# Two-block transformer kernel: the input rows of the first layer are scaled on ScalarE instead of VectorE

## Chip, core and metric

The kernel runs on one core of a Trainium2 chip. The metric is device time of one execution in microseconds. A row of the profile names engines as PE (TensorE), PEld (TensorE's weight loads), DVE (VectorE), ACT (ScalarE), POOL (GpSimd) and SP (the engine that issues the DMAs).

## What is computed

Two blocks follow each other on 1024 tokens of width 1024. The first has two layers. Its layer 0, where the change is, works on the 1024 rows of `x` and 256 context rows `ctx`:

```
hx = rms_norm(x, norm_g[layer]) * (1.0 + scx[:, None, :]) + shx[:, None, :]
hc = rms_norm(ctx, norm_g[layer]) * (1.0 + scc) + shc
...
ox, oc = even_mixer(hx, hc, ...)        # window attention with sinks, differential attention
x = x + gtx[:, None, :] * (ox @ w_out[layer])
```

with

```
def rms_norm(x, g):
    xf = x.astype(jnp.float32)
    y = xf * lax.rsqrt(jnp.mean(xf * xf, axis=-1, keepdims=True) + EPS)
    return (y * g.astype(jnp.float32)).astype(x.dtype)
```

`scx` and `shx` come from the condition through `adaln_params`. Layer 1 is gated linear attention. The second block mixes an LRU, a forgetting attention and an RWKV group, and ends with a gated feed-forward. All data are fp32.

## The kernel before

Rows are cut into tiles of 128: eight of `x` (t = 0 to 7) and two of `ctx` (t = 8, 9). Matrix products are made of fp32r halves: `split` (lines 99 to 106) casts a tile to a high part and subtracts it for the low part, and `mm3` (lines 126 to 134) runs three matmuls for each of eight slices of 128 (L132, L133, L134).

For each of the ten tiles `in_rows` (line 262) loads the rows into `x` (L266), squares two halves on ScalarE with a running sum (L270), adds the two sums on VectorE (L272), and calls `rsqrt`: multiply and add on VectorE (L95), power -0.5 on GpSimd (L97). L274 multiplies the whole 128x1024 tile by that value, in place. `in_T` (line 277) transposes it on TensorE in two halves (L258), evicts with the adaLN scale and shift, on ScalarE for the first half (L289) and on VectorE for the second (L287), and splits into `hT` (the cast, L105 on VectorE or L103 on ScalarE) and `lo` (L106 on GpSimd). The buffers `xt` are two, shared with `jk`, the output of the squares.

`keys_values` (line 548) multiplies a tile's `hT` with the first weights (`whi`, `wlo`; result in `mm`), norms and rotates the keys (`kn`, L358 to L375), transposes them (L382) and stores `kT` and `v`. `window_group` (line 466) takes four head pairs over the ten tiles: `proj_qg` makes q and its gate (`gs`, L430, L431), then scores (L394), row maxima (L400), exponentials (L601), transposed weights (L408, L410), and the sum over values (L615). The first four input tiles (8, 9, 0, 1) are prepared in `build`, between the adaLN products (L149 to L161); the rest by `ready` as pair 0 reaches them. Later adaLN parts (L179, L182, L187) run on ScalarE and GpSimd beside the window attention. `differential_group` follows. Line 249 in `norm_rows` is a scaling like L274 that already runs on ScalarE; it is used much later.

Nobody writes the order of instructions by hand here: the tile framework is called with its scheduler on (`schedule_with_timeline_sim=True`), which lays out each engine's queue from its own estimate of durations. Each engine then takes its queue strictly in that order. So an edit of one instruction can change the order on all engines, and in stages that follow.

Of the kernel before, what the change touches and what calls it, by code (L numbers as in the profile page):

```python
# [15 lines left out]
AF = mybir.ActivationFunctionType  # L16
ALU = mybir.AluOpType
# [14 lines left out]
class Builder:  # L32
# [229 lines left out]
    def in_rows(self, t):  # L262

        nc, I = self.nc, self.I
        x = self.adp.tile([128, 4, 256], F32, tag="x", name="x").rearrange("p a b -> p (a b)")
        nc.sync.dma_start(x, I["x"][t * 128:(t + 1) * 128] if t < 8 else I["ctx"][(t - 8) * 128:(t - 7) * 128])  # L266
        ss, rs = self.sums()
        jk = self.adp.tile([128, 512], F32, tag="xt", name="jk", bufs=XT)
        for half in range(2):
            nc.scalar.activation(jk, x[:, half * 512:half * 512 + 512], AF.Square, accum_out=ss[:, half:half + 1])  # L270
        rs = rs[:, :1]
        nc.vector.tensor_tensor(rs, ss[:, 0:1], ss[:, 1:2], op=ALU.add)  # L272
        self.rsqrt(rs, rs, 1.0 / 1024, EPS, 1)
        nc.vector.tensor_scalar(x, x, rs, None, op0=ALU.mult)  # L274
        return x

    def in_T(self, t, x, mds):
# [1788 lines left out]
```

## Time and profile before

| | us |
|---|---|
| median of 3 runs | 3123.26 |
| lowest, highest | 3115.8, 3126.36 |
| profiled execution, own time | 3118.71 |
| span of that execution | 3116.9 |
| TensorE busy | 2994.9 (96%) |
| VectorE busy | 2001.0 (64%) |
| ScalarE busy | 1451.7 (47%) |
| GpSimd busy | 749.7 (24%) |

The first tile's squares begin at 13.5 us, the last scaling of L274 at 130.0 us; the last value product of the window attention (L615) begins at 426.4 us. In the rows below, times are microseconds from the start of the span. A timeline row gives start, duration, engine, line, operation, output and inputs, and in brackets the idle time just before it and who ended it.

### The profile page before, as it was taken

What the parts mean: (1) busy time and instruction counts of PE and PEld (TensorE: products, weight loads), DVE (VectorE), ACT (ScalarE), POOL (GpSimd) and SP (SyncE); (2) the same over time, 40 slices, a digit from 0 to 9 for tenths busy, and PEclk for the clock granted to TensorE, in tenths of its full rate; (3) what the DMA queues carried; (4) which work ended last, traced back from release to release, by engine and by line L of the source; (5) the groups of instructions that cost most, each with busy time, mean ns of one, the idle gap of its engine ahead of it and who ended that gap; (6) DMA issues with size and microseconds to landing.
All of it is one profiled execution on the core that took longest, in us unless ns stands there. A gap on an engine that the chain in (4) does not pass through costs nothing.

```text
span 3116.9 us, 54778 instructions
## 1 busy us (share of the span) xinstructions
PE 2994.9 (96%) x20419; PEld 2729.3 (88%) x20419; DVE 2001.0 (64%) x5219; ACT 1451.7 (47%) x3605; POOL 749.7 (24%) x812
## 2 busy tenths in 40 slices
PE   8899999999999999999999999999998899999999
PEld 5799999889888789998788989888877899999887
DVE  5677757777776665446546543576645999998443
ACT  4689845555563553223236221245644444444332
POOL 2467621332220000000000000111002666663000
PEclk9999999999999999999999999899999999999999
DMA  5222210100033231112321121312232222223562
GB/s 216 61 87 85 93 41 5 33 28 13 15 129 115 87 111 58 50 56 85 122 84 48 51 71 56 89 47 60 71 111 82 68 82 89 82 82 114 175 198 95
DMA packets 164138, 253.00 MB, mean 81 GB/s; under 512 B 25800, under 2 KB 93440, under 8 KB 163872
## 3 DMA queue, kind: packets, MB, share of 16 engines
q1 hardware_dynamic: 163872, 249.50, 25.0%
q8 instruction: 161, 2.64, 0.4%
q14 instruction: 105, 0.86, 0.1%
HBM read 194.94 MB, written 54.51 MB: 80 GB/s over the span
## 4 chain that ended last, share of the span: by engine, by line
PE 80%; DVE 8%; DMA 4%; ACT 4%; issue 2%; POOL 1%; SPq 0%; DVEq 0%; POOLq 0%; ACTq 0%
PE mm L132 12%; PE mm L133 12%; PE mm L134 12%; PE dn L1788 8%; PE mm L1708 4%; PE mm L1707 4%; PE mm L1709 4%; PE te L408 3%; PE po L1537 3%; PE sc L394 3%; PE po L664 2%; PE po L615 2%; DVE upl L106 1%; ACT EB L649 1%; PE sc L885 1%
## 5 line engine op out<-in xcount | busy, mean ns | idle before, releaser
L132 PE MATMUL mm<-whi,hT 128*128 128x256 f32 (+1 forms) x1760 | 514.6, 293 | 18.4 <-DVE gs L431 5.4
L133 PE MATMUL mm<-wlo,hT 128*128 128x256 f32 (+1 forms) x1760 | 507.6, 289 | 1.9 <-POOL wlo L106 1.9
L132 PEld LDWEIGHTS mm<-whi,hT 128*128 128x128 f32 x1760 | 337.9, 192 | 26.2 <-DVE gs L431 5.6
L133 PEld LDWEIGHTS mm<-wlo,hT 128*128 128x128 f32 x1760 | 338.1, 192 | 5.3 <-POOL wlo L106 2.5
L134 PE MATMUL mm<-whi,lo 128*128 128x256 f32 x1040 | 301.1, 290 | 0.9 <-POOL lo L106 0.8
L97 POOL TENSOR_TENSOR inv<-inv,cm 128x1 f32<-128x1 f32 (+1 forms) x87 | 50.4, 580 | 1029.3 <-DVE inv L95 1029.3
L1653 POOL TENSOR_TENSOR uptmp<-upraw 128x256 f32<-128x256 f32 x220 | 216.2, 1011 | 231.9 <-DMA upraw<-in_ffn_up 219.0
L132 PE MATMUL mm<-hT,whi 128*128 128x352 f32 (+3 forms) x640 | 220.4, 345 | 2.8 <-ACT a L1021 1.8
L97 POOL TENSOR_TENSOR c<-c,cm 128x2 f32<-128x2 f32 (+1 forms) x170 | 126.3, 744 | 401.1 <-DVE c L95 355.6
L133 PE MATMUL mm<-hT,whi 128*128 128x352 f32 (+3 forms) x640 | 218.8, 342 | 0.1
L134 PE MATMUL mm<-hT,wlo 128*128 128x352 f32 (+3 forms) x640 | 218.6, 343 | 0.0
L410 ACT COPY wT<-te 128x512 f32<-128x512 f32 (+2 forms) x368 | 159.0, 453 | 121.0 <-PE te L408 110.8
L134 PE MATMUL mm<-whi,hT 128*128 128x256 f32 (+3 forms) x720 | 205.5, 286 | 0.0
L134 PEld LDWEIGHTS mm<-whi,lo 128*128 128x128 f32 x1040 | 202.3, 195 | 3.2 <-POOL lo L106 1.5
L1811 DVE SCALAR_TENSOR_TENSOR fy<-fx,ffnc,fy 128x512 f32<-128x512 f32 x176 | 135.7, 793 | 15.1 <-ACT fy L1809 15.1
L400 DVE TENSOR_SCALAR_CACHE_REDUCE EB<-sc 128x512 f32<-128x512 f32 (+1 forms) x208 | 120.0, 585 | 35.9 <-PE sc L394 33.1
L182 POOL TENSOR_TENSOR adacc<-adacc,adpr 128x512 f32<-128x512 f32 (+1 forms) x112 | 128.6, 1148 | 47.8 <-ACT adpr L179 32.3
L103 ACT CAST whi<-wraw 128x512 fp32r<-128x512 f32 (+2 forms) x120 | 84.0, 718 | 118.9 <-PE mm L133 45.4
L394 PE MATMUL sc<-kT,qTh 128*128 128x256 f32 (+2 forms) x352 | 125.8, 372 | 13.3 <-DVE EB L400 6.6
L1788 PE MATMUL dn<-dnl,fh 128*128 128x512 f32 x352 | 137.3, 390 | 0.0
L1788 PE MATMUL dn<-dnh,fl 128*128 128x512 f32 x352 | 137.2, 391 | 0.0
L134 PEld LDWEIGHTS mm<-whi,hT 128*128 128x128 f32 (+1 forms) x720 | 135.7, 188 | 1.4
(544 smaller groups left out, 9078.2 us busy)
## 6 DMA issues: line engine op xcount, KB each, us to landing
adraw<-in_adaln_w SPq DMA_DIRECT2D x48, 512.0 KB, 3.7
upraw<-in_ffn_up SPq DMA_DIRECT2D x44, 512.0 KB, 3.8
dnraw<-in_ffn_down SPq DMA_DIRECT2D x88, 256.0 KB, 3.4
wraw<-in_w_ab SPq DMA_DIRECT2D x26, 512.0 KB, 3.7
woraw<-in_w_out SPq DMA_DIRECT2D x48, 256.0 KB, 2.9
wraw<-in_w_gla SPq DMA_DIRECT2D x48, 256.0 KB, 2.8
wraw<-in_w_in SPq DMA_DIRECT2D x24, 512.0 KB, 4.2
fd<-fy SPq DMA_DIRECT2D x44, 256.0 KB, 2.5
```

What stands on the lines that cost most here:

```text
L97: nc.gpsimd.tensor_tensor(out, out, self.cm05[:p, :n], op=ALU.pow)
L132: mmul(ps, ah, bh, start=k == 0, stop=False)
L133: mmul(ps, ah, bl, start=False, stop=False)
L134: mmul(ps, al, bh, start=False, stop=k == nk - 1)
L182: nc.gpsimd.tensor_tensor(a, a, pr[:, :conds], op=ALU.add)
L394: self.nc.tensor.matmul(sp, q[x][:, m], keys, start=x == 0, stop=last and x == 1)
L410: nc.scalar.copy(w[:n, :m, :nq], ps.rearrange("p (j t) -> p j t", j=4)[:n, :m, :nq])
L1653: nc.gpsimd.tensor_tensor(tmp[:, qs], src, raw[:, h2, :, 128 * r2:128 * r2 + 128], op=ALU.add if sign > 0 else ALU.subtract)
L1707: nc.tensor.matmul(ps, wh, th, start=k == 0, stop=False)
L1708: nc.tensor.matmul(ps, wh, tl, start=False, stop=False)
L1788: nc.tensor.matmul(banks[t][i], a[e], b[g], start=k == 0 and n == 0, stop=k == 21 and n == 2)
L1811: nc.vector.scalar_tensor_tensor(y, x[part][:, :, tap:tap + 256], cw[:, tap, c:c + 1], y, op0=ALU.mult, op1=ALU.add)
```

## The change

L274 is one instruction. It was a `tensor_scalar` multiplication on VectorE; it becomes an activation with the function Copy and the per-row scale on ScalarE. Data, buffers and the steps around it stay.

```
@@ -271,7 +271,7 @@
         rs = rs[:, :1]
         nc.vector.tensor_tensor(rs, ss[:, 0:1], ss[:, 1:2], op=ALU.add)
         self.rsqrt(rs, rs, 1.0 / 1024, EPS, 1)
-        nc.vector.tensor_scalar(x, x, rs, None, op0=ALU.mult)
+        nc.scalar.activation(x, x, AF.Copy, scale=rs)
         return x
```

The order of instructions moves in four stretches: the whole window attention (762 of TensorE's rows), a few rows early in the differential attention, the forgetting attention of the second block (345 rows), and the start of the feed-forward (28 rows).

First place: ScalarE, between the adaLN products and the first keys. `xt` and `te` belong to the input tiles, `whi<-wraw` is a cast of weights, `adr` an adaLN row. Piece of the difference:

```order
 L289 ACTIVATE xt<-te,md_195 128x128 x2
 L289 ACTIVATE xt<-te,md_257 128x128 x2
+L274 ACTIVATE x<-x,inv 128x1024
 L103 CAST whi<-wraw 128x1024
 L152 COPY adr<-mm 2x512
+L103 CAST hT<-xt 128x4x128
 L103 CAST whi<-wraw 128x1024
-L103 CAST hT<-xt 128x4x128 x2
+L103 CAST hT<-xt 128x4x128
```

The scaling of tile 1 comes in ahead of a weight cast, and the first of two `hT` casts moves ahead of the next weight cast.

Second place: TensorE, after the keys of tile 1 (`mm_632`). `mm_677` and `mm_805` are q and gate of tiles 0 and 1, `te_736` and `te_748` the transposes of tile 2's rows `x_725`, `mm_760` tile 2's keys. Before:

```order
L134 MATMUL mm_632<-whi_205,lo11_122 128x256
L258 MATMUL te_736<-ident_r_68,x_725 128x128 x4
L258 MATMUL te_748<-ident_r_68,x_725 128x128 x4
L132 MATMUL mm_677<-whi_398,hT_118 128x256
L133 MATMUL mm_677<-wlo_399,hT_118 128x256
L134 MATMUL mm_677<-whi_398,lo00_119 128x256
```

And now:

```order
L134 MATMUL mm_677<-whi_404,lo01_120 128x256
L382 MATMUL tp_626<-ident_r_68,kn_612 128x128 x2
L258 MATMUL te_736<-ident_r_68,x_725 128x128 x4
L258 MATMUL te_748<-ident_r_68,x_725 128x128 x4
L382 MATMUL tp_671<-ident_r_68,kn_657 128x128 x2
L132 MATMUL mm_760<-whi_199,hT_118 128x256
L133 MATMUL mm_760<-wlo_200,hT_118 128x256
L132 MATMUL mm_805<-whi_398,hT_118 128x256
```

Tile 2's transposes moved behind the 24 matmuls of `mm_677`, and its keys were interrupted after two matmuls by `mm_805`.

Third place: TensorE in the forgetting attention, beside the RWKV group (`ra`). Before:

```order
L1184 MATMUL ra_21811<-X_21776,B_21378 128x128 x4
L1512 MATMUL sc_23874<-fkh_23776,fqh_23774 128x400
L1513 MATMUL sc_23874<-fkc0_23760,fql_23775 128x400
L1537 MATMUL po_23813<-fv_23783,wT_23816 16x64
L408 MATMUL te_23838<-ident_r_68,fE_23800 128x128
L1190 MATMUL ra_21834<-XT_21709,Y_21809 128x128 x4
```

And now:

```order
L1184 MATMUL ra_21811<-X_21776,B_21378 128x128 x4
L1537 MATMUL po_23813<-fv_23783,wT_23816 16x64
L408 MATMUL te_23838<-ident_r_68,fE_23800 128x128
L1512 MATMUL sc_23874<-fkh_23776,fqh_23774 128x400
L1513 MATMUL sc_23874<-fkc0_23760,fql_23775 128x400
L1190 MATMUL ra_21834<-XT_21709,Y_21809 128x128 x4
```

The same matmuls stand there; the scores of one query tile moved behind the value product of an earlier one.

## Rows read from the trace of the kernel before

**Rows 1.** The page: busy times, and the chain that ended last by engine.

```profile
PE 2994.9 (96%) x20419; PEld 2729.3 (88%) x20419; DVE 2001.0 (64%) x5219; ACT 1451.7 (47%) x3605; POOL 749.7 (24%) x812
...
PE 80%; DVE 8%; DMA 4%; ACT 4%; issue 2%; POOL 1%; SPq 0%; DVEq 0%; POOLq 0%; ACTq 0%
```

**Rows 2.** Busy us by stretch: from:to, length, PE, PEld, DVE, ACT, POOL, clock, DMA.

```profile
0.00:436.00 436.00, 401.16 (x3092) 370.47 (x3093) 287.96 (x1068) 309.31 (x957) 224.13 (x219) 0.97 0.31 102
...
1990.00:2320.00 330.00, 320.56 (x2204) 273.34 (x2204) 204.72 (x750) 170.25 (x420) 37.55 (x41) 0.95 0.28 77
...
48.00:61.00 13.00, 9.68 (x46) 9.41 (x47) 12.14 (x24) 7.03 (x25) 8.79 (x8) 0.63 0.53 175
61.00:75.00 14.00, 13.11 (x106) 12.58 (x105) 11.07 (x34) 6.94 (x32) 5.89 (x8) 0.98 0.13 43
75.00:100.00 25.00, 19.96 (x142) 18.62 (x142) 17.64 (x71) 15.24 (x51) 8.31 (x9) 0.91 0.15 46
100.00:135.00 35.00, 30.85 (x239) 29.24 (x238) 24.02 (x95) 20.73 (x71) 10.24 (x12) 0.97 0.13 44
```

**Rows 3.** TensorE's longest waits for VectorE, 0 to 200 us: total us, times, longest.

```profile
PE mm L132 <- DVE gs L431: 5.4, 3, 3.6
PE sc L394 <- DVE EA L400: 3.2, 2, 1.9
PE tp L382 <- DVE kn L358: 2.7, 1, 2.7
```

**Rows 4.** Line 274 by form (busy us, mean ns, idle before); line 249 (ns min/median/max).

```profile
L274 DVE TENSOR_SCALAR x<-x,inv 128x1024 f32<-128x1024 f32 x10 | 7.5, 753 | 5.4 <-POOL inv L97 5.4
...
L249 ACT ACTIVATE xs<-x,inv x9: 1147/1152/1153, 2298.1 to 2396.1; 128x1024 f32<-128x1024 f32 x8, 16x1024 f32<-16x1024 f32 x1
```

**Rows 5.** Timeline, end of tile 4's second square on ScalarE and its scaling.

```profile
84.70 0.19 ACT L270 ACTIVATION_READ_ACCUMULATOR jk<-x 128x1 f32 x1
...
85.94 0.75 DVE L274 TENSOR_SCALAR x<-x,inv 128x1024 f32<-128x1024 f32 x1 [0.67 <-POOL inv L97]
```

**Rows 6.** Timeline, 42 to 58 us: tiles 8 and 9, then kn.

```profile
42.82 1.37 DVE L287 TENSOR_SCALAR xt<-te,md 128x128 f32<-128x128 f32 x4
...
45.12 1.04 ACT L103 CAST whi<-wraw 128x1024 fp32r<-128x1024 f32 x1 [3.42 <-DMA wraw<-in_w_ab]
46.07 1.14 ACT L103 CAST hT<-xt 128x512 fp32r<-128x512 f32 x2
...
46.74 0.38 PE L132 MATMUL mm<-whi,hT 128*128 128x256 f32 x1 [1.84 <-ACT hT L103]
...
57.56 0.41 PE L382 MATMUL tp<-ident_r,kn 128*128 128x128 f32 x2 [2.72 <-DVE kn L358]
...
46.76 3.02 POOL L106 TENSOR_TENSOR lo<-xt,hT 128x512 fp32r<-128x512 f32 x2 [7.09 <-ACT hT L103]
53.45 1.73 POOL L106 TENSOR_TENSOR lo<-xt,hT 128x512 fp32r<-128x512 f32 x1 [3.67 <-DVE c L95]
...
55.93 0.29 DVE L375 TENSOR_TENSOR jk<-mm,c 128x128 f32<-128x128 f32 x1 [0.60 <-POOL c L97]
```

**Rows 7.** Timeline, tile 2 from its scaling to hT, and TensorE's wait at 73.78.

```profile
62.32 0.75 DVE L274 TENSOR_SCALAR x<-x,inv 128x1024 f32<-128x1024 f32 x1 [0.73 <-POOL inv L97]
...
65.27 1.04 PE L258 MATMUL te<-ident_r,x 128*128 128x128 f32 x8
...
67.83 0.42 DVE L105 CAST hT<-xt 128x512 fp32r<-128x512 f32 x1
...
73.78 0.35 PE L132 MATMUL mm<-whi,hT 128*128 128x256 f32 x1 [0.80 <-DVE gs L431]
```

**Rows 8.** ScalarE's longest wait in total, 40 to 135 us.

```profile
ACT jk L347 <- PE mm L134: 15.4, 8, 4.1
```

**Rows 9.** TensorE's two longest waits, 1990 to 2300 us.

```profile
PE ra L1213 <- ACT bn L1301: 3.0, 1, 3.0
PE sc L1512 <- DVE fkh L1480: 2.8, 1, 2.8
```

More of the change, by code (lines that the diff above doesn't have):

```diff
@@ L273, in in_rows @@
         self.rsqrt(rs, rs, 1.0 / 1024, EPS, 1)
-        nc.vector.tensor_scalar(x, x, rs, None, op0=ALU.mult)
+        nc.scalar.activation(x, x, AF.Copy, scale=rs)
         return x
```

## Prediction, made before the changed kernel ran

> **What bounds the kernel now.** I read the page first. TensorE is busy 96% of the span and carries 80% of the chain that ended last; VectorE carries 8%, ScalarE 4% [rows 1]. So an edit on VectorE or ScalarE counts only where TensorE waits for one of them, or where it moves TensorE's own work. The table by stage says where that can be. The ten edited instructions run between 16 and 130 us, inside the window attention of the first layer, which fills the first 436 us; TensorE idles 436 - 401.2 = 34.8 us of these [rows 2]. The list of TensorE's waits up to 200 us names whom it waited for: VectorE's lines 431, 400 and 358 for 11.3 us in all [rows 3]. The edited line 274 is in no row of it: TensorE never waited for a scaled row directly. What the edit can do goes through the queues of VectorE and ScalarE, and through the order in which the scheduler, which sees other durations, now lays out all engines.
>
> **What is removed.** Ten multiplications of 128x1024 on VectorE, 753 ns each, 7.5 us together. Before them VectorE sat 5.4 us idle in eight waits for the power on GpSimd, since the product stands straight behind the sum and the scaled mean that feed it [rows 4]. So VectorE gets back up to 7.5 + 5.4 = 12.9 us, of which the four early tiles (up to 40 us) are worth nothing: there TensorE works through the adaLN products and comes to the transposes later than their rows are scaled.
>
> **What is added.** Ten activations with a per-row scale on ScalarE. The trace has the same form, out of the same kind of buffers, at line 249: 1152 ns [rows 4]. That is 11.5 us, 0.40 us more than on VectorE for each tile. The order lists hold these ten more instructions on ScalarE and nothing else, so no table load comes with them. The wait for the power moves too. From the end of the second square's accumulator (84.70 + 0.19 = 84.89) to the scaling (85.94) it is 1.05 us on an idle VectorE [rows 5]. On ScalarE the scaling of three of the ten tiles (3, 6 and 7) stands straight behind its own squares, and blocks the queue for about those 1.05 us; the casts of q, the square sums of the keys and the exponentials stand behind it. The other seven have work in between.
>
> By the Trainium skill (ScalarE: Activation LUTs, Rules for kernel authors) a plain multiplication belongs on VectorE, and the two durations of [rows 4] agree for the single instruction. If each tile's extra 0.40 us were on the path the sum would be 4.0 us worse; the forecast's own terms below do not use this.
>
> **What moves, first place: 44 to 58 us.** Before, ScalarE's first hT cast waits behind a weight cast whose data land at 45.12. TensorE runs dry at 46.74 - 1.84 = 44.90 and starts again at 46.74; GpSimd then makes the two low halves in 1.51 us each, and TensorE stops 2.72 us more until VectorE's kn lets it go on at 57.56 [rows 6]. In the new order the first cast stands ahead of the weight cast. Its input is evicted half way through the row of 42.82, at about 43.5; with 0.57 us for the cast and 1.51 us for the low half tile 8 continues at about 45.6. Tile 9 still needs the weight cast, its own cast and its low half: 45.12 + 1.04 + 0.57 + 1.51 = 48.2. But all that TensorE then does is to reach the wait for kn earlier, and VectorE's list of work ahead of kn is the same as before. One thing changes there: the hT cast of tile 0 moves ahead of two evictions and two table products, so GpSimd's 1.73 us subtraction behind it ends sooner, by more than the 0.60 us for which line 375 waited on the power queued behind that subtraction. Gain: this 0.60 us, not the 1.84 us that a list of waits suggests.
>
> **Second place: 61 to 75 us.** Before, tile 2's row is scaled by 62.32 + 0.75 = 63.07 us, transposed from 65.27 on, and its hT cast ends at 67.83 + 0.42 = 68.25, 2.98 us after the transposes began [rows 7]. Now ScalarE scales it behind the square sums of tile 0's keys, and on TensorE the transposes stand 24 matmuls and two transposes later. A matmul takes 13.11 / 106 = 0.124 us in this stretch [rows 2]: 24 x 0.124 = 3.0, with the pair 3.2 us. So the transposes begin at 65.3 - 0.6 + 3.2 = 67.9 and hT is there at 70.9. TensorE has done the transposes (1.04 us) and the next pair (0.41) by 69.3 and waits 1.6 us for it. The wait of 0.80 us at 73.78 goes with the old order. Cost: 0.8 us. The two places together leave +0.2 us.
>
> **The other five tiles, 75 to 135 us.** VectorE gets 5 x (0.75 + 0.67) = 7.1 us back; ScalarE takes 5 x 1.15 + 3 x 1.05 = 8.9 us more. Both have room on average: in these 60 us ScalarE is idle 24.0 us and VectorE 18.3 us [rows 2]. Most of ScalarE's idle time is waiting for TensorE's products, 15.4 us between 40 and 135 us in eight waits of up to 4.1 us [rows 8], and that is what covers the added work. I take 0, with -7.1 and +8.9 as ends. If the cover is gone, the scaling is late for tp and scores and costs its 1.15 us a tile.
>
> **Later stages.** What the ramp has won or lost by 135 us is passed on: every stage after it is TensorE's [rows 1]. The forgetting attention of the second block has no edited instruction, but the scheduler ordered 345 of TensorE's rows there differently. Between 1990 and 2320 us TensorE idles 9.4 us, mostly in two waits of 3.0 and 2.8 us [rows 2, 9]. Such waits can vanish or come again: 0, with -5.8 and +5.8. The feed-forward start has 28 rows moved; I take 0.
>
> **Sum.** The profiled execution took 3118.71 us with a span of 3116.9. +0.2 makes 3118.9. The median of the three runs is 3123.26, 4.55 us above it, so the prediction is 3123.5 us. A measurement of this kernel tells about 0.3%, 9.4 us, from no change; the runs of before lie between 3115.8 and 3126.36.
>
> **The rivals.** (a) *ScalarE becomes the bound, slower.* Place: tiles 3 to 7, where casts of q and exponentials queue behind a scaling that waits for GpSimd. Price: 8.9 us there and 0.8 us at tile 2 without the gain at the first place, 9.7 us: 3133 us. It decides where ScalarE's scaling ends later than TensorE's products, so that the waits for TensorE [rows 8] turn round. For it: 1152 against 753 ns, three scalings straight behind their squares. Against: ScalarE's 24 us idle. The skill's rule above would have it so. (b) *VectorE was the bound, faster.* The 11.3 us that TensorE waited for VectorE's three lines [rows 3] shrink by what tiles 2 to 7 free, 6 x 1.42 = 8.5 us, and 0.6 us at kn: 9.1 us, 3114 us. It reaches further if the gap goes: from 48 to 61 us, after it, the granted clock is 0.63, that is mostly the lower level of 1.2 GHz, and 46 matmuls take 9.68 us, 0.210 us each against 0.124 us in the next stretch [rows 2]; that is 46 x 0.086 = 4.0 us: 3110 us. Against: the new order leaves a gap there too. (c) *The new order decides, not the edit.* The forgetting attention alone gives 3123.5 +- 5.8: 3118 or 3129 us, within what can be told. (d) The change not doing what it says is out: the order lists have the ten on ScalarE and none on VectorE.
>
> **How the numbers follow.** Forecast with (c): 0.77. (a) 0.13, (b) 0.10. The likeliest gives 3123.5. The ends -0.6 - 7.1 - 5.8 = -13.5 and +0.8 + 8.9 + 5.8 = +15.5 will hardly fall together; three quarters of them, -10.1 and +11.6, give 3113 to 3135 us, which takes in (a) and the near end of (b) and leaves no more than 2 in 10 out. Faster by over 0.3%: 0.10; within: 0.77; slower: 0.13.
>
> **What would show it.** Line 274 on ScalarE at about 1150 ns, ten times, none on VectorE. TensorE's wait for hT at 46.7 us shorter, the one for kn still there but ending near 57.0 us; a new wait of 1 to 3 us for an hT cast near 70 us; TensorE's idle time up to 436 us within 7 us of 34.8; 9 +- 6 us between 1990 and 2320. Wrong if ScalarE's line 274 turns up ahead of casts that TensorE waits for (a), if TensorE's waits for lines 431, 400 and 358 fall by more than half (b), or if a stage that holds no edited instruction moves by over 9 us.

## The result, and the profile after

| | before | changed |
|---|---|---|
| median, 18 runs each | 3120.62 us | 3139.05 us |
| lowest to highest | 3110.83 to 3131.06 | 3122.43 to 3151.85 |
| ratio, 95% interval | | 1.0060 (1.0046 to 1.0075) |
| profiled execution: span | 3116.9 us | 3146.2 us |

The changed kernel is slower by 0.6%, 18 us of the median. The forecast was 3123.5 us, no change, with a range of 3113 to 3135 us. Its profiled execution is 29.3 us longer than that of before. The page of after, its busy line and its chain, which answer to [rows 1]:

```profile
PE 3012.2 (96%) x20419; PEld 2742.9 (87%) x20419; DVE 1985.8 (63%) x5209; ACT 1463.4 (47%) x3615; POOL 750.6 (24%) x812
...
PE 82%; DVE 7%; DMA 4%; ACT 3%; issue 2%; POOL 1%; SPq 1%; DVEq 0%; POOLq 0%; ACTq 0%
```

VectorE is busy 15.2 us less (7.5 us of it are the ten scalings), ScalarE 11.7 us more. TensorE issues the same 20419 instructions and is busy 17.3 us longer with them. That is the first thing to see: of the 29.3 us of this execution 17.3 are not idle time, they are the same work taking longer. Line 274 now stands on ScalarE, with the duration read at line 249 (min/median/max in ns):

```profile
L274 ACT ACTIVATE x<-x,inv x10: 1131/1150/1159, 17.3 to 136.7; 128x1024 f32<-128x1024 f32 x10
```

By stage, the same stretches as in [rows 2] (length, busy us of PE, PEld, DVE, ACT, POOL, granted clock, DMA):

```profile
0.00:436.00 436.00, 395.38 (x3044) 363.74 (x3044) 268.16 (x1043) 318.30 (x959) 222.76 (x216) 0.96 0.30 101
1990.00:2320.00 330.00, 318.69 (x2126) 273.36 (x2126) 191.13 (x721) 159.13 (x395) 33.27 (x33) 0.90 0.26 68
48.00:61.00 13.00, 7.94 (x46) 7.30 (x45) 10.56 (x25) 6.16 (x23) 9.02 (x7) 0.74 0.60 210
61.00:75.00 14.00, 11.85 (x86) 11.37 (x86) 7.84 (x30) 8.36 (x30) 5.35 (x7) 0.88 0.12 39
75.00:100.00 25.00, 20.32 (x146) 19.41 (x145) 13.38 (x56) 13.99 (x45) 6.49 (x8) 0.86 0.06 22
100.00:135.00 35.00, 28.25 (x210) 25.89 (x209) 19.85 (x80) 22.44 (x68) 11.12 (x12) 0.95 0.16 52
```

Idle time of TensorE is 436 - 395.4 = 40.6 us in the window attention (34.8 before) and 330 - 318.7 = 11.3 us in the second window (9.4 before). The granted clock of the latter went from 0.95 to 0.90, and 78 fewer matmuls fit in it.

Where the 29.3 us came in, by marks that both traces have. L615 is the value product of the window attention, L1512 the first matmul of the scores of the forgetting attention, L1708 stands at the start of the feed-forward part and L1788 at its end. The last L615 starts at 435.2 us (426.4 before, +8.8). From there to the first L1512 of the forgetting attention both take 1585.0 us, with 8.8 us still between them. From the first L1512 to the first L1708 of the feed-forward part it is 400.1 us after 378.8 (+21.3), and from there to the last L1788 718.5 after 719.3 (-0.8). So the larger part of the loss of this execution came in a stage in which no instruction was edited. That stage, from mark to mark, in one row each (PE busy, count, clock), before and then changed:

```profile
2011.40:2390.20 378.80, 375.43 (x2460) 320.32 (x2461) 227.64 (x796) 190.89 (x465) 39.26 (x47) 0.97 0.27 78
```

```profile
2020.20:2420.30 400.10, 394.52 (x2462) 336.13 (x2462) 226.36 (x796) 190.83 (x465) 39.93 (x47) 0.92 0.26 74
```

The same number of matmuls to within two; idle time 3.4 and 5.6 us; busy time 19.1 us longer, at a mean clock of 0.92 for 0.97. In rows of 5 us a stretch without a change stands at one of two levels, 1.00 (2.4 GHz) or 0.50 (1.2 GHz). From the changed kernel (PE busy, count, clock, DMA):

```profile
2146.00:2151.00 5.00, 5.00 (x39) 1.00 0.52 117
2151.00:2156.00 5.00, 5.00 (x24) 0.72 0.40 96
2156.00:2161.00 5.00, 5.00 (x19) 0.50 0.01 3
...
2201.00:2206.00 5.00, 0.77 (x2) 0.84 0.57 146
2206.00:2211.00 5.00, 5.00 (x23) 0.50 0.48 151
...
2226.00:2231.00 5.00, 5.00 (x20) 0.50 0.17 52
2231.00:2236.00 5.00, 5.00 (x41) 0.92 0.24 77
```

Two falls. The second, from about 2204 to 2232, comes with a wait. The first, from about 2153 to 2174, follows on none: TensorE is busy for all of the 48 us ahead of it and all through it.

```profile
2104.60:2153.20 48.60, 48.60 (x354) 1.00 0.23 58
2153.20:2173.70 20.50, 20.50 (x85) 0.50 0.02 7
```

Before, there is one fall in this part, and it ends after about 10 us. (Ahead of these, both kernels stand at 0.50 for the first 13 to 14 us of the stage.)

```profile
2181.00:2186.00 5.00, 3.86 (x23) 0.85 0.89 260
2186.00:2191.00 5.00, 5.00 (x23) 0.50 0.66 196
2191.00:2196.00 5.00, 5.00 (x23) 0.62 0.21 74
2196.00:2201.00 5.00, 5.00 (x37) 1.00 0.32 105
```

The wait at 2205 in the timeline of the changed kernel, ScalarE's rows and then TensorE's:

```profile
2203.17 0.62 ACT L103 CAST wo<-woraw 128x512 fp32r<-128x512 f32 x1 [4.59 <-DMA woraw<-in_w_out]
...
2204.83 1.27 ACT L410 COPY wT<-te 16x128 f32<-16x128 f32 x4
...
2205.13 0.95 PE L408 MATMUL te<-ident_r,fE 128*16 128x128 f32 x2 [4.27 <-ACT wT L410]
```

A cast of the output weight (`wo`) stands ahead of the copies of the transposed exponentials (`wT`) on ScalarE, and waits 4.59 us for its DMA. Before, casts of this weight waited too (0.74 and 0.47 us), but they and the copies stood so that TensorE lost 0.94 and 0.20 us. The trace therefore gives a first reading: the new order, not the edit, and the clock more than the waits. The experiments test it.

### The profile page after: what moved, and what is told of

Read it like the earlier page. It is cut to its first block, busy times and chain, and to the rows that moved or that the text cites. A ratio compares the mean times of both kernels' runs of the same rounds, so it can differ in the third digit from the quotient of the medians.

```text
span 3146.2 us, 54777 instructions
## 1 busy us (share of the span) xinstructions
PE 3012.2 (96%) x20419; PEld 2742.9 (87%) x20419; DVE 1985.8 (63%) x5209; ACT 1463.4 (47%) x3615; POOL 750.6 (24%) x812
## 4 chain that ended last, share of the span: by engine, by line
PE 82%; DVE 7%; DMA 4%; ACT 3%; issue 2%; POOL 1%; SPq 1%; DVEq 0%; POOLq 0%; ACTq 0%
PE mm L132 12%; PE mm L133 12%; PE mm L134 12%; PE dn L1788 8%; PE mm L1707 4%; PE mm L1708 4%; PE mm L1709 4%; PE te L408 3%; PE po L1537 3%; PE sc L394 3%; PE po L664 2%; PE po L615 2%; DMA woraw<-in_w_out 1%; ACT EB L649 1%; PE sc L1512 1%
## 5 line engine op out<-in xcount | busy, mean ns | idle before, releaser
L1788 PE MATMUL dn<-dnl,fh 128*128 128x512 f32 x352 | 137.3, 390 | 0.0
L1788 PE MATMUL dn<-dnh,fl 128*128 128x512 f32 x352 | 137.2, 391 | 0.0
L394 PE MATMUL sc<-kT,qTh 128*128 128x256 f32 (+2 forms) x352 | 126.2, 371 | 10.4 <-DVE EB L400 6.7
```

Of the source, the lines that this page charges most:

```text
L394: self.nc.tensor.matmul(sp, q[x][:, m], keys, start=x == 0, stop=last and x == 1)
L1788: nc.tensor.matmul(banks[t][i], a[e], b[g], start=k == 0 and n == 0, stop=k == 21 and n == 2)
```

## Experiments

### Engine or order: four kernels

The edit changes two things at once: the engine of ten instructions, and the order in which the scheduler, which sees other durations, issues the rest. A function added behind the tracing holds every engine's instructions (all but the ten) to a table of positions, read off from one kernel's order and used in the other (the packed table is written here as `ORDER`, the list of engines as `ENGINES`):

```diff
+def fix_order(nc, tc):
...
+    for e, row in zip(ENGINES, ORDER):
...
+            if prev is not None:
+                tc.add_manual_dep(ins, prev.name, nosync, reason="fixed order")
+            prev = ins
...
     with tile.TileContext(nc, schedule_with_timeline_sim=True) as tc:
         tile_blocks(tc, aps, out)
+        fix_order(nc, tc)
```

The edges bind the order of issue alone. In all that follows "early" is the program up to the second block's mixer (what differs there is nearly all in the window attention), "late" the forgetting attention and what follows.

**act_old_order**: the changed kernel, held to the order of before.

> The ten scalings run on ScalarE as in the changed kernel, but every engine's other instructions are held in the order of the kernel before (edges that cost no wait). It takes the order out and leaves the engine. Engine theory (ten scalings of 1.15 us for 0.75 us, some of them just behind their own squares on ScalarE, are what costs): the end of the window attention stays late by about 9 us (435 for 426 us), and the time stays near the changed kernel's, 3139 us or a ratio of about 1.006. Order theory (the new order of the other engines' work is what costs): the window attention ends within 3 us of 426.4, the forgetting attention between its first and its last L1512 takes the 258 us of before, and the time is within 6 us of 3120.6, ratio 0.998 to 1.002.

**dve_new_order**: the kernel before, held to the order of the changed one.

> The reverse: the scalings stay on VectorE as in the kernel before, and every engine's other instructions are held in the order of the changed kernel. Engine theory: the time is the kernel before's, 3120.6 us, ratio 0.998 to 1.002, with the window attention's end at 426 to 429 us. Order theory: the time is near the changed kernel's, ratio 1.004 to 1.007, with the end of the window attention 5 to 9 us late and 280 us for 258 between the first and the last L1512. If both count, it lies between, about 1.003.

**dve_new_late**: the kernel before, held to its own order early and to the changed kernel's late.

> The scalings on VectorE and the order of the kernel before up to the end of the second mixer's start (the window attention is untouched); only from the forgetting attention on does the order of the changed kernel hold. It tells whether the 21.6 us that the profiled run of the changed kernel lost in the forgetting attention belong to the order there. Order theory: the forgetting attention takes 10 to 22 us longer than before and the ratio is 1.003 to 1.007. Clock theory (those 21.6 us are stretches at the 1.2 GHz level that come and go from run to run with any order): the ratio is 0.999 to 1.001 with a spread of runs like the kernel before's (20 us).

**act_new_early**: the changed kernel, held to its own order early and to that of before late.

> The changed kernel with its own order up to the forgetting attention, and from there on the order of the kernel before. If the window attention and the forgetting attention add up, this has the window attention's 9 us alone: ratio about 1.003, window attention ending at 435, the forgetting attention at 258 us between the first and the last L1512. Clock theory (a late arrival by itself brings the 1.2 GHz stretches of the forgetting attention, whatever the order there): 280 us there and a ratio of 1.006.

Measured, with the two marks of each trace:

| kernel | engine | early order | late order | ratio (95%) | last L615 | first L1512 to first L1708 |
|---|---|---|---|---|---|---|
| before | VectorE | old | old | 1 | 426.4 | 378.8 |
| act_old_order | ScalarE | old | old | 1.0013 (1.0003 to 1.0023) | 428.6 | 375.6 |
| act_new_early | ScalarE | new | old | 1.0021 (1.0011 to 1.0032) | 432.1 | 381.0 |
| dve_new_late | VectorE | old | new | 1.0046 (1.0031 to 1.0062) | 426.0 | 387.5 |
| dve_new_order | VectorE | new | new | 1.0069 (1.0037 to 1.0102) | 436.2 | 414.9 |
| changed | ScalarE | new | new | 1.0060 (1.0046 to 1.0075) | 435.2 | 400.1 |

The marks are those of one execution each, and some of these stand at an end of their kernel's range: dve_new_order's took 3162.05 us (its runs 3125.96 to 3163.49), act_old_order's 3113.26 (3113.26 to 3126.62), dve_new_late's 3126.77 (3126.77 to 3138.11). So the ratios tell what an order costs, and the marks where. That the edges by themselves cost nothing is seen in two kernels further down, which are held to the order of before but for a few instructions: 1.0006 and 0.9996.

The order theory holds. With the edit taken back and the order kept, the loss is all there; with the edit kept and the order taken back, 0.13% is left, 4 us (0.9 to 7.2). Under the new order the runs can't tell the engines apart (1.0069 and 1.0060). The late order alone costs 0.46%, 14 us (9.7 to 19.3), the largest share; early order and engine together cost 0.21%, and 0.46 + 0.21 = 0.67 comes near the 0.60 of the whole. The clock theory, that the stretches at 1.2 GHz in the forgetting attention come and go with any order alike, is out: dve_new_late differs from before in its late order alone, and its ratio is 1.0046 (1.0031 to 1.0062) where that theory asked for 0.999 to 1.001. In its trace, of its fastest run, the stage is 8.7 us longer, less than the 10 to 22 us that were expected; 8.5 of these are busy time.

The early part, 80 to 120 us, in rows of before, the changed kernel, dve_new_order and act_old_order (one fence each; PE busy, count, clock):

```profile
80.00:120.00 40.00, 34.48 (x251) 0.91 0.12 38
```

```profile
80.00:120.00 40.00, 29.77 (x201) 0.87 0.13 42
```

```profile
80.00:120.00 40.00, 29.62 (x199) 0.87 0.13 42
```

```profile
80.00:120.00 40.00, 32.83 (x236) 0.91 0.13 42
```

The new order idles 10.2 us here with ScalarE and 10.4 with VectorE, the old one 7.2 and 5.5. (Three more kernels with the new order early, act_new_early among them, show 8.2 to 8.6.) The rows on which it does so, of the changed kernel and of dve_new_order:

```profile
84.50 0.35 PE L132 MATMUL mm<-whi,hT 128*128 128x256 f32 x1 [3.34 <-DVE hT L105]
...
109.86 1.10 PE L258 MATMUL te<-ident_r,x 128*128 128x128 f32 x8 [2.24 <-ACT x L274]
```

```profile
85.41 0.36 PE L132 MATMUL mm<-whi,hT 128*128 128x256 f32 x1 [3.34 <-DVE hT L105]
...
110.54 1.09 PE L258 MATMUL te<-ident_r,x 128*128 128x128 f32 x8 [1.91 <-DVE aM L591]
```

The wait at 109.86 names the edited line, and looks like proof against ScalarE. The second fence shows the same wait, 0.33 us shorter and under another name, with the scaling on VectorE. The row comes late because the new order has tile 5's squares on ScalarE at 106.15 us, behind two exponentials; before they started at 98.63, ahead of them. A releaser's name in a trace tells which instruction was last, not what made it late.

### Halves of the window attention

**new_to_75** and **old_to_75** are the changed kernel with its own order up to the transposes of tile 3 and that of before behind it, and the reverse; both have the old order late.

> Scalings on ScalarE, the changed kernel's order up to the transposes of the sixth row tile (78.7 us there), the order of before from there on: the first two places of the prediction alone. TensorE's idle time up to 440 us is the measure (before 34.8, the changed kernel 42.2, ScalarE with the old order 36.5). If those places came out as predicted (+0.2 us net), it is 36 to 38 us and 80 to 120 us holds 6 to 8 us of idle as in the old order; if the early places bring the loss, 40 to 42.

> The complement: scalings on ScalarE, the order of before up to the transposes of the sixth row tile, then the changed kernel's order to the end of the window attention, then the order of before. If the stretch of tiles 3 to 7 (set at nothing in the forecast) is where the window attention loses, the idle time up to 440 us is 40 to 42 us, with about 10 us of it between 80 and 120 us; if not, 36 to 38 us.

Idle time up to 440 us came out as 38.6 and 36.1 us. A second trace of the kernel before gave 31.9 us for the 34.8 of the first (again_before, below), so these sums tell little by themselves. The stretch of 80 to 120 us is steadier: 6.0 us of idle with the old order there and 10.0 with the new, as expected for the place of that loss. The last L615 starts at 431.5 and 432.7 us, later than the 428.6 of act_old_order and near the 432.1 to 436.1 of the traces with the whole new order on ScalarE. Both halves seem to share in the loss, but marks that differ by 4 us under one order don't divide it: on the sum the pair is inconclusive.

### The wait for the output weight's cast

**late_casts_new**: the changed kernel in its own order but for four instructions.

```diff
 ScalarE
-L103 CAST wo<-woraw
 L1525 ACTIVATE fE<-fE,fnM
-L103 CAST wo<-woraw
 L410 COPY wT<-te            (five of these)
+L103 CAST wo<-woraw
+L103 CAST wo<-woraw
```

> The changed kernel in its own order, but for one place in the forgetting attention: on ScalarE two casts of the output weight (L103 wo<-woraw) stand behind the five L410 copies that they stood ahead of, and on VectorE their two subtractions stand behind the next maxima. In the changed kernel the first of these casts waits 4.59 us for its DMA with the copies queued behind it, TensorE waits 4.27 us for the copies, and 25 us at the 1.2 GHz level follow. If that place is what the new order costs there, the wait for wT goes under 1 us, the stretch after it goes or shrinks to the 10 us of before, the time from the first L1512 to the first L1708 falls from 400 us to 380 to 388, and the ratio from 1.006 to 1.002 to 1.004. If the casts only name the last releaser and something else is late there, the wait stays at 2 us or more under another name, and the ratio at 1.006.

Measured: 1.0065 (1.0041 to 1.0090), no gain. The wait fell from 4.27 to 2.46 us; it moved to the next cast that waits for its DMA. And the fall of the clock that no wait explains was there again, and longer:

```profile
2146.00:2151.00 5.00, 5.00 (x39) 1.00 0.49 120
2151.00:2156.00 5.00, 5.00 (x23) 0.72 0.37 93
...
2186.00:2191.00 5.00, 5.00 (x21) 0.50 0.05 13
2191.00:2196.00 5.00, 5.00 (x25) 0.69 0.06 16
```

So the reading that this one cast is what the late order costs falls: the ratio of 1.002 to 1.004 that it asked for lies outside the interval. What the place would cost without any wait isn't shown, since 2.46 us of it stayed.

**late_casts_old**: the kernel before, held to its own order, with the same repair at its casts near 2180 us (four casts behind the copies, and VectorE's four subtractions behind the next maxima).

> The kernel before (scalings on VectorE, its own order) with the same repair: the casts of the output weight that stand ahead of the L410 copies near 2182 us, where TensorE waits 0.94 and 0.20 us for wT and some 10 us at the 1.2 GHz level follow, stand behind these copies. If a stretch at 1.2 GHz follows on these waits alone, it goes, the time falls by 5 to 7 us, ratio 0.998. If the waits before it (0.29 for fE, 0.92 for fo) already bring it on, the clock falls as before and the time stays within 2 us of 3119.

Measured: 1.0006 (0.9991 to 1.0021). The waits of 0.94 and 0.20 us for wT went, one of 1.78 us for fo (line 1538, where VectorE reads the sums out) came in their place, and the clock fell as before, in the profiled execution for more than 45 us without a gap:

```profile
2200.00:2245.00 45.00, 45.00 (x193) 0.50 0.15 49
```

193 matmuls in 45 us, 0.233 us each; in the row at 2196 of before it is 5.00 / 37 = 0.135 us. Two things follow. This repair of the one place doesn't beat the kernel before. And a long stretch at 1.2 GHz can come with nearly the old order as well: that execution took 3138.19 us, where the other runs in the interval took 3113.15 to 3123.53. By these runs an order changes how often such a stretch comes, and doesn't switch it.

### Which heads, and a second trace of each kernel

**new_heads_1_5** and **new_heads_6_8**: the changed kernel, early order its own; late order its own up to the sixth head's first matmul and that of before behind it, and the reverse.

> The changed kernel with its own order up to the first matmul of the sixth of the eight heads of the forgetting attention, and the order of before from there on: it keeps the stretch near 2150 us, where the clock fell with TensorE busy, and takes away the wait of 4.3 us for wT near 2205 us. If the stretch near 2150 is what the new order brings, the clock falls there again, the heads 5 and 6 start over 35 us apart (39 to 48 in three traces with the whole new order, 31.5 before), and the ratio is 1.004 to 1.006. If the wait near 2205 is, the ratio is that of the old order from the forgetting attention on, 1.002, with 29 to 32 us between those two heads.

> The complement: the order of before from the forgetting attention's start to the first matmul of its sixth head, then the changed kernel's order, with the wait for wT behind the output weight's cast. If that wait and the 20 to 25 us at 1.2 GHz behind it are the cost, the heads 6 and 7 start 42 us apart (33 before) and the ratio is 1.004 to 1.005; if the stretch near 2150 is, 1.002 to 1.003 here. If both count, both runs lie between 1.003 and 1.005.

The wait near 2205 us lies in the fifth head, not in the sixth as the expectations have it, so the first of these kept it (3.1 us). Measured: 1.0125 (1.0105 to 1.0145) and 1.0044 (1.0031 to 1.0056). The first is slower than the whole new order, and where the two orders meet TensorE waits 3.3 us more for fE (the exponentials), with the clock at 1.2 GHz again behind it; but it has the fall near 130 us into the stage, and the second, with the old order in these heads, doesn't. Set beside act_new_early's 1.0021, the sixth to eighth heads bring 0.23% with waits of their own (1.4 us for frl, the reciprocal of the row sums, and 0.9 for wT).

**again_after** and **again_before**: the two kernels once more, unchanged.

> The changed kernel once more, for a second trace. Order theory: the places at which TensorE waits come back within 1 us (84.5, 109.9 and 2205 us after the same start), since the order sets them. What does not come back at the same place is the clock's: the fall near 2150 us, with no wait before it, should be there in some runs only if it is what spreads this kernel's times over 30 us.

> The kernel before once more, for a second trace: its idle time of TensorE up to 440 us within 1.5 us of 34.8, the window attention's end within 2 us of 426.4, and from the first L1512 to the first L1708 379 us if its clock falls as it did, up to 20 us more if the fall near 2182 us lasts longer, as in the run with the casts moved (399 us).

again_after: 1.0063 (1.0033 to 1.0093), last L615 at 434.6 us. The early waits came back within 1 us of their places (10.3 us of idle between 80 and 120 us). The wait for wT in the fifth head came back too, 3.8 us, but 6 us earlier (2199.2), since the clock's fall ahead of it did not: near 2150 us it stays at 1.00, and there is a shorter one some 55 us earlier, with TensorE busy for the 38 us ahead of it, so that the stage takes 385.5 us for 400.1:

```profile
2020.40:2405.90 385.50, 380.82 (x2462) 324.52 (x2462) 225.94 (x796) 190.34 (x465) 39.86 (x47) 0.96 0.25 76
```

again_before: 3114.11 us in one run, 378.3 us for the stage (378.8), last L615 at 426.1. So in two traces the old order repeats itself within 1 us at these marks (its idle time up to 440 us did not come within the 1.5 us that were expected: 31.9 for 34.8), and the new one spreads by 15 us almost through the clock alone: its idle time is 4.7 us here, 5.6 in the first trace. In this second pair of traces the forgetting attention isn't the larger part: 8.5 us come in up to the last L615 and 7.2 us in the stage.

### What in the fourth head brings the clock down

Between 2139 and 2154 us, where the clock falls in the changed kernel, its order issues no score matmul of 256 columns or more, because it puts the two pairs of one tile (400 and 512 columns) next to each other. **score_pair_back** moves the second pair to where before has it; **score_pair_early** moves it forward in the kernel before.

```diff
 TensorE (changed kernel)
 L1512, L1513 MATMUL sc<-fkh,fqh / fkc,fql   400 columns
-L1512, L1513 MATMUL sc<-fkh,fqh / fkc,fql   512 columns
 ...                                         (18 instructions)
+L1512, L1513 MATMUL sc<-fkh,fqh / fkc,fql   512 columns
```

> The changed kernel with two matmuls moved, no more: in the fourth head of the forgetting attention the L1512 and L1513 with 512 columns of one score tile, which the new order issues straight behind those with 400 columns at 2138.76 us, go 20 matmuls later, where the order of before has them. In the changed kernel no score matmul of 256 columns or more then runs for 14.7 us (119 to 134 us into the stage; at most 8.9 us before), and the clock falls in that stretch while TensorE is busy. Theory of the narrow stretch: without it the fall near 2150 us is gone or rarer, the time from the first L1512 to the first L1708 goes from 400 and 385 us in two traces to 383 to 388, the ratio from 1.006 to 1.003 to 1.004. Rival, that the fall hangs on when the stage starts and not on these rows: fall and ratio stay, 1.006.

> The reverse in the kernel before: the same two matmuls, 512 columns, go 25 matmuls earlier, straight behind those with 400, and nothing else moves. By the theory of the narrow stretch (14 us without a wide score matmul in place of 8.6) the clock now falls in some runs near 2135 us with TensorE busy: the ratio goes to 1.002 to 1.005 with a wider spread of the runs. By the rival the time stays within 0.1% of before.

Measured: 1.0080 (1.0048 to 1.0112) and 0.9996 (0.9984 to 1.0008). Both against the theory. With the pair back the clock fell at the same place; with the pair early, 13.7 us without a wide score matmul, it stayed up. In 10 us stretches, score_pair_back and then score_pair_early:

```profile
2135.00:2145.00 10.00, 8.73 (x68) 1.00 0.01 2
2145.00:2155.00 10.00, 10.00 (x47) 0.58 0.47 107
2155.00:2165.00 10.00, 10.00 (x35) 0.50 0.00 0
```

```profile
2135.00:2145.00 10.00, 10.00 (x70) 1.00 0.43 104
2145.00:2155.00 10.00, 10.00 (x82) 1.00 0.04 13
```

The theory of the narrow stretch as the sole cause falls. (In score_pair_back the moved pair made a wait of 1.3 us just ahead of the fall, so that this run alone would not decide; the other half has no such fault.)

**old_to_fifth_head** and **new_to_fifth_head** repeat the cut of the heads one head earlier, between the fourth head's stretch and the wait for wT.

> The changed kernel's order up to the forgetting attention, the order of before to the fifth head's first matmul (2189 us in the changed kernel), then the changed kernel's order, so that the wait for wT near 2205 us is kept and the narrow stretch of the fourth head is not. The earlier pair of runs was cut one head later than I took it to be, so that both places stood in one of them. If the wT wait is worth its 4 us and half of the 20 to 25 us at 1.2 GHz behind it, less the 10 us at 1.2 GHz that before has there: 8 to 10 us over the old order's 1.002, ratio 1.005. If it is the narrow stretch alone, 1.002 to 1.003.

> The complement: the changed kernel's order to the fifth head's first matmul, then the order of before. It has the narrow stretch of the fourth head and the old order around the output weight's casts. If the stretch is the cost: a fall at about 130 us after the first L1512, ratio 1.004 to 1.007. If the wT wait is: 1.002 to 1.003. Where the two orders meet a wait of 1 to 4 us may come in, as it did in the earlier pair.

Measured: 1.0051 (1.0031 to 1.0072) and 1.0057 (1.0037 to 1.0078). Against 1.0021 for the old order in all heads, each half costs 0.3% or more, and together they would make more than the whole's 0.60; the meeting of two orders has its price again, so the division isn't clean. new_to_fifth_head shows a fall about 130 us into the stage; old_to_fifth_head's trace shows the wait (4.8 us), no more lost to the clock than before (0.97), and 381.4 us for the stage, but that run was one of its fastest (3125.86 us of 3122.3 to 3146.89).

**What stays open.** Eight traces have the new order in the first four heads. From 130 to 150 us after the first L1512 the clock is 0.58 in that of the changed kernel, 0.56 in dve_new_order and late_casts_new, 0.57 in new_heads_1_5, 0.53 in score_pair_back and 0.65 in new_to_fifth_head; TensorE is busy for 20 us and more ahead of the fall in all but score_pair_back. In again_after and dve_new_late it is 1.00. Ten traces have the old order there, and all show 1.00. So the fall was seen only with the new order of these heads. All six traces that have it have the new order early as well, and the one trace with the old order early has it not, so that the early order may have to be new too. Which rows do it, or what in the time of arrival decides, none of the runs settles.

## Why the prediction was wrong, point by point

**What is removed and added: right.** 1150 ns on ScalarE where 1152 was taken; ScalarE waited 4.4 us for the power, in five scalings, where three of 1.05 us were taken. Engine alone, order held: +0.13%, 4 us (0.9 to 7.2). The sentence on the Trainium skill's rule (ScalarE: Activation LUTs, Rules for kernel authors) put the ten at 4.0 us worse if all of it were on the path; the measurement agrees with that size, though no row shows it as ten times 0.40: act_old_order's waits grow at v (1.5 us for 0.6) and kn (3.8 for 2.7) and shrink at gs (2.3 for 5.4).

**First place: right in kind, mis-sized.** The wait for the casts went, the wait for kn stayed, as forecast. tp came at 56.04 us, 1.5 us earlier than before, where the term was 0.60:

```profile
46.74 0.38 PE L134 MATMUL mm<-whi,lo 128*128 128x256 f32 x1 [0.47 <-POOL lo L106]
49.70 0.39 PE L134 MATMUL mm<-whi,lo 128*128 128x256 f32 x1 [1.27 <-POOL lo L106]
...
56.04 0.66 PE L382 MATMUL tp<-ident_r,kn 128*128 128x128 f32 x2 [2.77 <-DVE kn L358]
```

**Second place: the wait right, its price wrong.** Forecast were the transposes at 67.9, hT at 70.9 and a wait of 1.6 us. In the trace:

```profile
66.54 0.28 PE L132 MATMUL mm<-whi,hT 128*128 128x256 f32 x1
...
67.47 1.04 PE L258 MATMUL te<-ident_r,x 128*128 128x128 f32 x8
...
71.10 0.58 PE L132 MATMUL mm<-whi,hT 128*128 128x256 f32 x1 [1.81 <-DVE hT L105]
...
72.34 0.41 PE L132 MATMUL mm<-whi,hT 128*128 128x256 f32 x1
```

67.47, 71.10 and 1.81 us. But the last row shows what the sum left out: behind the wait the matmuls take 0.41 for 0.28 us and follow on each other every 0.21 us for 0.12. The clock had gone to 1.2 GHz. The stretch 61 to 75 us went from 0.98 [rows 2] to 0.88, which is 0.10 x 14 = 1.4 us, more by itself than the 0.8 us that the place was priced at; idle time went from 0.9 to 2.2 us besides.

**Tiles 3 to 7: wrong.** Taken as 0, because ScalarE had idle time to cover its new work. ScalarE's time was not the question. The new order put squares behind exponentials and a cast of hT where TensorE comes to it too early, and between 80 and 120 us that costs 3.0 us of idle time with ScalarE (10.2 for 7.2) and 4.9 with VectorE (10.4 for 5.5); the engine, in the old order, costs 1.7. Over the 75 to 135 us of the forecast TensorE idles 11.4 us for 9.2. The ends, -7.1 and +8.9, held it; the value didn't.

**Later stages: the step that failed.** "0, with -5.8 and +5.8" for the forgetting attention, from two waits that "can vanish or come again". By its idle time this was right: 11.3 us in 1990 to 2320, where the test named 9 +- 6. But over all runs the late order alone costs 14 us (9.7 to 19.3), beyond the bound. The bounds counted idle time alone. Of the 21.3 us in the first trace, 2.2 are idle and 19.1 the same matmuls at a lower clock; in the second trace 1.3 and 5.4, in all 6.7; in dve_new_late 0.2 and 8.5. The profile of before had shown the price: in its own fall, 2181 to 2195, and in [rows 2], where 48 to 61 us stood at 0.63. I used that row for rival (b) alone, as something to be won, and not for what 345 moved rows might lose. The same holds for the range: its -5.8 and +5.8 had no row with the clock in them.

**The sum and the rivals.** Window attention: +0.2 us forecast, +8.8 at the last L615 of the trace. 48 to 135 us idle 18.6 us for 13.4, and lose about 10.3 us to the clock for 8.4 (each stretch by what its clock lacks to 1.00), by [rows 2] and the same rows of after. The idle time up to 436 us, 40.6 us, still lies within the 7 us of 34.8 that the forecast's test named. The base was 2.6 us high: a median of three runs, 3123.26, where 18 give 3120.62. Rival (a), 3133 us, was nearest in time, but by the wrong mechanism: ScalarE is not the bound, and the engine costs 4 us (0.9 to 7.2) where it named 9.7. Rival (b) fails: with VectorE freed and the order held nothing was won. The waits for lines 431, 400 and 358 are 9.7 us there for 11.3, and 6.5 in the changed kernel, not less than half, with others in their place. Rival (c), the order decides and not the edit, was the mechanism, and what the forecast put 0.77 on, with its size bounded far too low. The last line of the forecast's tests, a stage without an edited instruction that moves by over 9 us, is what came true in the first trace (21.3; in the second it is 6.7).

## What to carry to other kernels

Where a scheduler lays out the program anew, an edit of 4 us can move the whole by 18: ask of every stage whose rows moved what its waits could become, and hold the order fixed to learn what the edit itself is worth. Price a wait of TensorE with the clock behind it: a stage that already shows a stretch at 1.2 GHz in the kernel before, as this one did, can show more and longer ones, and a bound that sums waits alone is too narrow. And where a wait names the edited line, look for the same wait in a kernel without the edit before the line is blamed.

## What the runs showed of the hardware

The granted clock fell to 1.2 GHz without any idle time of TensorE ahead of it: at 2153 us of the changed kernel TensorE had been busy for 48.60 of 48.60 us, and was busy all through the fall, and in late_casts_old the clock stayed at 0.50 for 45 us of unbroken matmuls. (Busy is the profile's word; it models the ends of matmuls.) The Trainium skill (TensorE: Matmul & The Clock Gate, Why this matters for your kernels) advises against longer idle gaps between bursts of matmuls, since they bring the clock down. The row at 2205 us agrees with it (4.27 us of wait, then 0.50). At 71.10 us the clock fell behind a wait of 1.81 us, shorter than the gaps that the page names, and the falls near 2150 us happened without one.

The same program, traced twice, lost about 32 and 15 us from the first L1512 to the first L1708 to the clock (0.08 x 400.1 and 0.04 x 385.5), where the kernel before lost about 11 (0.03 x 378.8). The spread of the changed kernel's runs, 29 us for 20 of before, goes with it: among its 18 runs the time falls as the mean granted clock of the run rises, from 0.983 at 3122.43 us to 0.971 at 3149.68.
